# Last half of the rows in two column halves, and its stores on three queues

## The chip, the cores and the metric

The kernel runs on one core of one Trainium2 chip. The metric is device time of one execution in microseconds (us); less is better. Five engines run side by side and wait for each other by semaphores: TensorE (PE, matrix products; PEld are its weight loads), VectorE (DVE), ScalarE (ACT), GpSimd (POOL) and SyncE (SP, which only issues DMAs). ACT and POOL can issue DMAs too. All DMAs are carried by sixteen DMA engines.

## The reference

Two transformer layers in float32 on 256 rows of width 2048: a hybrid block (a matrix-memory LSTM and a gated delta rule) and then an attention block (differential attention and neighbourhood attention). What matters here is the very end of the second block:

```python
mixed = jnp.concatenate([oa, ob], axis=-1) @ w_out[layer]
h = h + gate[:, None] * mixed
return rmsnorm(h, final_g)
```

`mixed` is a product of 256 x 2048 by 2048 x 2048. `gate` is one number for each of the 2048 columns. `rmsnorm` divides each row by the root of its mean square over all 2048 columns, so no output of a row can be scaled before the whole row is there, and multiplies by `final_g`, one number for each column.

## The kernel before

The 256 rows are two halves `t` of 128 rows, which lie on the 128 partitions. The 2048 output columns are four blocks `n` of 512. The depth of 2048 is sixteen tiles `kt` of 128. Products are exact to float32 by splitting both operands into a high and a low part (`hi`, `lo`, type fp32r): each product is three TensorE instructions, high by high, high by low and low by high. The weight block of one `n` is loaded in eight pieces `q` of two depth tiles by `load_w` (lines 131 to 143): SyncE fetches the raw piece, ACT writes `hi` (line 139), DVE writes `lo` (line 140).

Column blocks 0 to 2 go through `proj` (lines 161 to 174): each piece is used for both row halves at once, so both are done at the same time. For block 3 (lines 1437 to 1455) all eight pieces of the weights are kept, five of them in buffers named `kept`, and each row half has a PSUM tile `pL` of 512 columns and 48 products of its own (16 depth tiles times three): first half `t = 0`, then `t = 1`. The first half's tail then runs while TensorE does the second half.

The tail of one row half is two functions. `last` (lines 1391 to 1397) multiplies the PSUM result by the gate (DVE, 1395), adds the residual (DVE, 1396) and squares the sum on ACT with a running total into one column of `s3t` (1397), a column for each block `n`. `store` (1399 to 1413) adds the four totals (DVE, 1402), turns them into a mean (DVE, 1403), takes the power -0.5 on POOL (`pow_`, line 178), and scales the four blocks of 512 columns by it: blocks 0 and 1 on ACT (1412), block 2 on DVE (1410), block 3 on DVE with `final_g` in the same instruction (1408; the others were multiplied by it before). Each block is stored by a DMA of 128 x 512 numbers, 256 KB, from SyncE (1413).

The order of the instructions on an engine is not that of the code: a scheduler sets it, with its own estimate of times, from the dependences. In the program before, it puts some products of the second row half among those of the first, where weights of the first are not ready by its estimate, and lets the stores leave in the order 2, 0, 1, 3. Each engine then keeps to its order.

Of the kernel before, what the change touches and what calls it, by code (L numbers as in the profile page):

```python
# [9 lines left out]
F32 = mybir.dt.float32  # L10
F32R = mybir.dt.float32r
AF = mybir.ActivationFunctionType
ALU = mybir.AluOpType
# [3 lines left out]
P = 128  # L17
D = 2048
T = 256
KT = D // P  # L20
# [64 lines left out]
def hybrid_block_kernel(  # L85
# [3 lines left out]
    nc = tc.nc  # L89
    act, ve, pe, gp = nc.scalar, nc.vector, nc.tensor, nc.gpsimd  # L90
    out = out[0]
# [10 lines left out]
    small = ctx.enter_context(tc.tile_pool(name="small", bufs=2))  # L102

    def side(shape=(P, 512), name="s"):
        return psB.tile(list(shape), F32, tag="s", name=name)
# [25 lines left out]
    def load_w(src, nk, ncol, hilo=None):  # L131
        raw = wraw.tile([P, nk, ncol], F32, tag="w", name="w")
        nc.sync.dma_start(raw, src)
        return split_w(raw, nk, ncol, hilo)

    def split_w(raw, nk, ncol, hilo=None):
        hi, lo = hilo or (wsp.tile([P, nk, ncol], F32R, tag=tg, name=tg) for tg in ("hi", "lo"))
        with tc.high_priority(offset=100):
            act.activation(hi, raw, AF.Copy)  # L139
            last_lo[0] = ve.tensor_tensor(lo, raw, hi.bitcast(F32), ALU.subtract)  # L140
        if tick[0] is not None:
            tick[0]()
        return hi, lo

    def proj_T(w, j0, ntiles, acts, name="pT"):

        na = len(acts)
        ps = psA.tile([P, 2, 2, T], F32, tag="p", name=name)
        for j in range(ntiles):
            for h in range(2):  # L150
                hi, lo = load_w(w[j0 + j, h], 8, P)
                for k in range(8):
                    kt = h * 8 + k
                    for a, (xh, xl) in enumerate(acts):
                        o = ps[:, a, j, :] if na == 2 else ps[:, j // 2, j % 2, :]
                        pe.matmul(o, hi[:, k, :], xh[:, kt, :], start=(kt == 0), stop=False)  # L156
                        pe.matmul(o, hi[:, k, :], xl[:, kt, :], start=False, stop=False)  # L157
                        pe.matmul(o, lo[:, k, :], xh[:, kt, :], start=False, stop=(kt == KT - 1))  # L158
        return ps

    def proj(w, n, acts, name="pN", qs=range(8), pss=None):

        pss = pss or [psA.tile([P, 2, 512], F32, tag="p", name=name) for _ in acts]
        for q in qs:
            hi, lo = load_w(w[n, q], 2, 512)
            for ps, (xh, xl) in zip(pss, acts):
                for t in range(2):
                    s = slice(t * P, (t + 1) * P)
                    for k in range(2):
                        kt = q * 2 + k  # L170
                        pe.matmul(ps[:, t, :], xh[:, kt, s], hi[:, k, :], start=(kt == 0), stop=False)  # L171
                        pe.matmul(ps[:, t, :], xh[:, kt, s], lo[:, k, :], start=False, stop=False)  # L172
                        pe.matmul(ps[:, t, :], xl[:, kt, s], hi[:, k, :], start=False, stop=(kt == KT - 1))  # L173
        return pss

    def pow_(o, i, e):

        gp.tensor_tensor(o, i, e, ALU.pow)
# [21 lines left out]
    with ExitStack() as b1:  # L200
# [17 lines left out]
        with ExitStack() as s0:  # L218
# [64 lines left out]
            for w in range(2):  # L283
                for j in (1, 3):
                    for h in range(2):
                        hl = load_w(d["dn_qkv"][J0[w] + j, h], 8, P)
                        o = ps0[w][:, j // 2, j % 2, :]
                        for k in range(8):
                            kt = h * 8 + k
# [50 lines left out]
        with s1:  # L340
            nc.sync.dma_start(raws, d["if_ba"])
            ps = side([P, T], name="ps")[0:48]
            for h in range(2):
                hi, lo = split_w(raws[:, h * 8:(h + 1) * 8, :], 8, 48)
                for k in range(8):
                    kt = h * 8 + k
# [20 lines left out]
            e = gpool.tile([P, 2, 24], F32, name="e")  # L367
# [118 lines left out]
        def gate_row(n):  # L486

            gate = macc[8 + n][0]
            bm = modp[0].tile([P, 512], F32, tag="m", name="bm", bufs=4)
            nc.sync.dma_start(bm, d["b_mod"][(8 + n) * 512:(9 + n) * 512].partition_broadcast(P))  # L490
            ps = side(name="ms")
            pe.matmul(ps, ones, gate, start=True, stop=True)
            ve.tensor_tensor(gate, bm, ps, ALU.add)
            return gate
# [14 lines left out]
        def mods_all(upto):  # L509
            while mod_next[0] < upto:  # L510
                mod_step(mod_next[0])
                mod_next[0] += 1
# [6 lines left out]
        with ExitStack() as s2:  # L519
# [44 lines left out]
            for hg in range(4):  # L564
                vv, ww = (dn.tile([P, 2, 4, P], F32, tag=nm, name=nm) for nm in ("vv", "ww"))
                kq = dk.tile([P, 4, 2, T], F32, tag="kq", name="kq")
                ps = kps0 if hg == 0 else proj_T(d["dn_qkv"], 16 + 4 * hg, 4, U)
                rows = rsb if hg == 0 else None
                conv_silu(ps, 16 + 4 * hg, kq[:, :, 0, :], rows)
                ps = qps0 if hg == 0 else proj_T(d["dn_qkv"], 4 * hg, 4, U)  # L570
# [63 lines left out]
                ps = proj_T(d["dn_qkv"], 32 + 4 * hg, 4, U)  # L634
# [93 lines left out]
                for t in range(2):  # L728
                    for h in range(4):
                        s = gz[:, t, h * P:(h + 1) * P]  # L730
# [15 lines left out]
        with ExitStack() as s3:  # L746
# [3 lines left out]
            for hg in range(2):  # L750
                kq = dk.tile([P, 4, 2, T], F32, tag="kq", name="kq")
                kT, qT = kq[:, :, 0, :], kq[:, :, 1, :]
                ps = proj_T(d["ml_k"], 4 * hg, 4, U)
                act.activation(kT, ps.rearrange("p a b t -> p (a b) t"), AF.Copy)  # L754
                ps = proj_T(d["ml_q"], 4 * hg, 4, U)
                act.activation(qT, ps.rearrange("p a b t -> p (a b) t"), AF.Copy, scale=P ** -0.5)
                for hp_ in range(2):
# [58 lines left out]
                    for b in range(2):  # L816
# [4 lines left out]
                        for j in range(2):  # L821
                            k = 4 * (2 * hg + hp_) + 2 * b + j
# [10 lines left out]
        hf = [hfp.tile([P, 2, 512], F32, tag="hf", name="hf", bufs=4) for _ in range(4)]  # L833
# [30 lines left out]
        with ExitStack() as s4:  # L864
# [66 lines left out]
            for n in range(4):  # L931
# [3 lines left out]
                for kk in range(4):  # L935
                    ps = side([P, T], name="ps")
                    for t in range(2):
                        pe.transpose(ps[:, t * P:(t + 1) * P], xs[:, t, kk * P:(kk + 1) * P], ident)
                    k = 4 * n + kk
# [10 lines left out]
    with ExitStack() as b2:  # L950
# [201 lines left out]
        a2 = b2.enter_context(tc.tile_pool(name="a2", bufs=2, reuse_waits="tile"))  # L1152
# [233 lines left out]

        M = [(Cat(mah, mbh), Cat(mal, mbl))]
        hf = []
        s3t = small.tile([P, 2, 4], F32, tag="s3t", name="s3t")
        r3 = small.tile([P, 2], F32, tag="r3", name="r3")  # L1390
        def last(ps, t, n, gate):

            h_ = hf[n][:, t, :]
            y = a2.tile([P, 512], F32, tag="e", bufs=3, name="y")
            ve.tensor_tensor(y, ps, gate, ALU.mult)
            ve.tensor_tensor(h_, h_, y, ALU.add)
            act.activation(y, h_, AF.Square, accum_out=s3t[:, t, n:n + 1])

        def store(t, fw):

            r = r3[:, t:t + 1]
            ve.tensor_reduce(r, s3t[:, t, :], AX.X, ALU.add)
            ve.tensor_scalar(r, r, 1.0 / D, 1e-6, ALU.mult, ALU.add)
            pow_(r, r, mh[:, 0:1])
            for n in range(4):
                h_ = hf[n][:, t, :]
                if n == 3:
                    ve.scalar_tensor_tensor(h_, h_, r, fw, ALU.mult, ALU.mult)
                elif n == 2:
                    ve.tensor_scalar(h_, h_, r, None, ALU.mult)  # L1410
                else:
                    act.activation(h_, h_, AF.Copy, scale=r)
                nc.sync.dma_start(out[t * P:(t + 1) * P, n * 512:(n + 1) * 512], h_)


        early = [proj(d["out2"], n, M, qs=range(4)) for n in range(2)]
# [2 lines left out]
        for n in range(4):  # L1419
            fw = a2.tile([P, 512], F32, tag="e", bufs=3, name="fg")  # L1420
            act.dma_start(fw, d["final_g"][n * 512:(n + 1) * 512].partition_broadcast(P))
            if n % 2 == 0:
                hv = a2.tile([P, 2, 2, 512], F32, tag="V", name="hv")
            hf.append(hv[:, n % 2])
            act.dma_start(hf[n], hd[n])
            for t in range(2):
                act.activation(hf[n][:, t, :], hf[n][:, t, :], AF.Copy, scale=r1[:, t:t + 1])
            mods_all(128 + 16 * (n + 1))
            gate = gate_row(n)
            if n < 3:  # L1430
                ps = early[n][0] if n < 2 else proj(d["out2"], n, M)[0]
                for t in range(2):
                    last(ps[:, t, :], t, n, gate)
                    gp.tensor_tensor(hf[n][:, t, :], hf[n][:, t, :], fw, ALU.mult)
                continue

            kept = []
            for _ in range(2):
                kv_ = a2.tile([P, 2, 2, 2, 512], F32R, tag="kT", name="kept")
                kept += [(kv_[:, i, 0], kv_[:, i, 1]) for i in range(2)]  # L1440
            qv = a2.tile([P, 2, 2, 512], F32R, tag="qT", name="kept", bufs=1)
            kept.append((qv[:, 0], qv[:, 1]))
            ws = [load_w(d["out2"][n, q], 2, 512, kept[q] if q < 5 else None) for q in range(8)]
            mh_, ml_ = M[0]
            for t in range(2):
                s = slice(t * P, (t + 1) * P)
                ps = side(name="pL")
                for q, (hi, lo) in enumerate(ws):
                    for k in range(2):
                        kt = q * 2 + k  # L1450
                        pe.matmul(ps, mh_[:, kt, s], hi[:, k, :], start=(kt == 0), stop=False)  # L1451
                        pe.matmul(ps, mh_[:, kt, s], lo[:, k, :], start=False, stop=False)
                        pe.matmul(ps, ml_[:, kt, s], hi[:, k, :], start=False, stop=(kt == KT - 1))
                last(ps, t, n, gate)
                store(t, fw)


# [54 lines left out]
```

## Time and profile before

| | |
|---|---|
| three runs | 1937.52, 1931.1, 1936.2 us |
| median | 1936.2 us |
| the profiled execution's own time | 1928.47 us |
| its span, first to last instruction | 1926.6 us |
| mean granted TensorE clock | 0.995 |
| TensorE busy | 1892.6 us, 98% of the span |
| VectorE busy | 1491.6 us, 77% |
| ScalarE busy | 928.7 us, 48% |
| GpSimd busy | 256.7 us, 13% |

Busy shares are averages over the whole span. Matrix products are pipelined: one begins while the one before is still on its way, so the distance of their starts, and not the length of one, is what they cost. Times in the rows are microseconds from the span's start. A DMA has three moments: its issue on a queue, its data's time on the sixteen engines, and its landing, when the semaphore is told.

### The profile page before, as it was taken

What the parts mean: (1) busy time and instruction counts of PE and PEld (TensorE: products, weight loads), DVE (VectorE), ACT (ScalarE), POOL (GpSimd) and SP (SyncE); (2) the same over time, 40 slices, a digit from 0 to 9 for tenths busy, and PEclk for the clock granted to TensorE, in tenths of its full rate; (3) what the DMA queues carried; (4) which work ended last, traced back from release to release, by engine and by line L of the source; (5) the groups of instructions that cost most, each with busy time, mean ns of one, the idle gap of its engine ahead of it and who ended that gap; (6) DMA issues with size and microseconds to landing.
All of it is one profiled execution on the core that took longest, in us unless ns stands there. A gap on an engine that the chain in (4) does not pass through costs nothing. (4 is left out here: it accounts for less than half of the span.)

```text
span 1926.6 us, 31678 instructions
## 1 busy us (share of the span) xinstructions
PE 1892.6 (98%) x12358; PEld 1676.7 (87%) x12358; DVE 1491.6 (77%) x2141; ACT 928.7 (48%) x1240; POOL 256.7 (13%) x371
## 2 busy tenths in 40 slices
PE   9999999999999999999999999999999999999997
PEld 9989898999878898888888887889999998988776
DVE  6978687684648999879995558698787768878976
ACT  7645444453434443444444356663333355555553
POOL 1011010101101221112120000000000023301311
PEclk9999999999999999999999999999999999999999
DMA  8555454454545778768887576663343387557975
GB/s 294 168 165 169 153 169 155 143 176 137 164 158 198 240 258 264 242 222 266 283 284 245 194 258 227 199 212 116 126 148 120 122 288 204 166 174 256 300 248 178
DMA packets 123974, 389.76 MB, mean 202 GB/s; under 512 B 15408, under 2 KB 21976, under 8 KB 123312
## 3 DMA queue, kind: packets, MB, share of 16 engines
q1 hardware_dynamic: 95296, 314.44, 48.7%
q0 software_dynamic: 19296, 54.19, 9.7%
q10 hardware_dynamic: 9232, 19.11, 2.9%
q8 instruction: 97, 1.59, 0.3%
q14 instruction: 53, 0.43, 0.1%
HBM read 368.50 MB, written 16.03 MB: 200 GB/s over the span
## 5 line engine op out<-in xcount | busy, mean ns | idle before, releaser
L139 ACT ACTIVATE hi<-w 128x1024 fp32r<-128x1024 f32 (+1 forms) x535 | 559.1, 1047 | 711.3 <-PE pN L173 393.5
L140 DVE TENSOR_TENSOR lo<-w,hi 128x1024 fp32r<-128x1024 f32 (+1 forms) x535 | 647.7, 1213 | 266.1 <-ACT hi L139 256.7
L172 PE MATMUL pN<-lo,uh 128*128 128x512 f32 x768 | 306.2, 399 | 0.0
L171 PE MATMUL pN<-hi,uh 128*128 128x512 f32 x768 | 304.7, 397 | 0.0
L173 PE MATMUL pN<-hi,ul 128*128 128x512 f32 x768 | 304.5, 396 | 0.0
L156 PE MATMUL pT<-uh,hi 128*128 128x256 f32 x896 | 255.5, 285 | 2.2 <-ACT kq L754 1.9
L158 PE MATMUL pT<-uh,lo 128*128 128x256 f32 x896 | 256.5, 286 | 0.0
L157 PE MATMUL pT<-ul,hi 128*128 128x256 f32 x896 | 255.7, 285 | 0.0
L171 PEld LDWEIGHTS pN<-hi,uh 128*128 128x128 f32 x768 | 145.0, 189 | 33.8
L173 PEld LDWEIGHTS pN<-hi,ul 128*128 128x128 f32 x768 | 145.0, 189 | 33.2
L172 PEld LDWEIGHTS pN<-lo,uh 128*128 128x128 f32 x768 | 145.1, 189 | 33.1
L156 PEld LDWEIGHTS pT<-uh,hi 128*128 128x128 f32 x896 | 168.7, 188 | 5.2 <-ACT kq L754 2.1
L158 PEld LDWEIGHTS pT<-uh,lo 128*128 128x128 f32 x896 | 168.8, 188 | 2.9 <-issue 2.4
L473 DVE SCALAR_TENSOR_TENSOR ma<-m,sc,ma 128x512 f32<-128x512 f32 x240 | 171.1, 749 | 0.0
L157 PEld LDWEIGHTS pT<-ul,hi 128*128 128x128 f32 x896 | 168.8, 188 | 1.8 <-issue 1.2
L463 POOL DMA_DIRECT2D m<-in_w_mod_dram x128 | 69.5, 543 | 287.7 <-DVE ma L473 206.1
L139 ACT ACTIVATE hi<-TT 128x1024 fp32r<-128x1024 f32 x56 | 59.6, 1065 | 77.2 <-PE pK L1064 54.6
L140 DVE TENSOR_TENSOR lo<-TT,hi 128x1024 fp32r<-128x1024 f32 x56 | 68.4, 1223 | 21.0 <-ACT hi L139 20.6
L156 PE MATMUL pT<-hxh,hi 128*128 128x256 f32 x256 | 73.7, 288 | 1.8 <-ACT ra L1165 1.8
L157 PE MATMUL pT<-hxl,hi 128*128 128x256 f32 x256 | 73.0, 285 | 0.0
L158 PE MATMUL pT<-hxh,lo 128*128 128x256 f32 x256 | 73.0, 285 | 0.0
L172 PE MATMUL pN<-lo,hxh 128*128 128x512 f32 x160 | 63.7, 398 | 1.9 <-DVE lo L140 1.8
(729 smaller groups left out, 4053.1 us busy)
## 6 DMA issues: line engine op xcount, KB each, us to landing
w<-in_dn_qkv_dram SPq DMA_DIRECT2D x88, 512.0 KB, 3.2
m<-in_w_mod_dram POOLq DMA_DIRECT2D x128, 256.0 KB, 4.1
w<-in_dn_z_dram SPq DMA_DIRECT2D x32, 512.0 KB, 3.2
w<-in_ml_v_dram SPq DMA_DIRECT2D x32, 512.0 KB, 3.8
w<-in_ml_z_dram SPq DMA_DIRECT2D x32, 512.0 KB, 4.2
w<-in_ml_o_dram SPq DMA_DIRECT2D x32, 512.0 KB, 4.1
w<-in_gate_a_dram SPq DMA_DIRECT2D x32, 512.0 KB, 4.4
w<-in_gate_b_dram SPq DMA_DIRECT2D x32, 512.0 KB, 4.4
```

The lines of the kernel that those rows point to most:

```text
L139: act.activation(hi, raw, AF.Copy)
L140: last_lo[0] = ve.tensor_tensor(lo, raw, hi.bitcast(F32), ALU.subtract)
L156: pe.matmul(o, hi[:, k, :], xh[:, kt, :], start=(kt == 0), stop=False)
L157: pe.matmul(o, hi[:, k, :], xl[:, kt, :], start=False, stop=False)
L158: pe.matmul(o, lo[:, k, :], xh[:, kt, :], start=False, stop=(kt == KT - 1))
L171: pe.matmul(ps[:, t, :], xh[:, kt, s], hi[:, k, :], start=(kt == 0), stop=False)
L172: pe.matmul(ps[:, t, :], xh[:, kt, s], lo[:, k, :], start=False, stop=False)
L173: pe.matmul(ps[:, t, :], xl[:, kt, s], hi[:, k, :], start=False, stop=(kt == KT - 1))
L463: (gp if g < 8 else nc.sync).dma_start(raw, d["w_mod"][g, kt])
L473: ve.scalar_tensor_tensor(a, raw, s, a, ALU.mult, ALU.add)
```

## The change

The second half of the rows (`t = 1`) of column block 3 is done in two halves of 256 columns, each with a PSUM tile, 48 products and a call of `last` of its own; the left half comes first in the code. `s3t` has five columns instead of four for each row half: the right half of `t = 1` writes the fifth, and GpSimd clears it at the start, since the first row half doesn't write it. In `store` the four blocks are scaled in the code's order 2, 0, 3, 1, and their DMAs are issued by SyncE (2 and 3), ACT (0) and POOL (1). This holds for both row halves.

```diff
-        s3t = small.tile([P, 2, 4], F32, tag="s3t", name="s3t")
+        s3t = small.tile([P, 2, 5], F32, tag="s3t", name="s3t")
+        gp.memset(s3t[:, :, 4:5], 0.0)
...
-        def last(ps, t, n, gate):
+        def last(ps, t, n, gate, cols=slice(0, 512), i=None):
...
-            h_ = hf[n][:, t, :]
-            y = a2.tile([P, 512], F32, tag="e", bufs=3, name="y")
-            ve.tensor_tensor(y, ps, gate, ALU.mult)
+            h_ = hf[n][:, t, cols]
+            y = a2.tile([P, 512], F32, tag="e", bufs=3, name="y")[:, cols]
+            ve.tensor_tensor(y, ps, gate[:, cols], ALU.mult)
             ve.tensor_tensor(h_, h_, y, ALU.add)
-            act.activation(y, h_, AF.Square, accum_out=s3t[:, t, n:n + 1])
+            i = n if i is None else i
+            act.activation(y, h_, AF.Square, accum_out=s3t[:, t, i:i + 1])
...
-            for n in range(4):
+            for n, q in ((2, nc.sync), (0, act), (3, nc.sync), (1, gp)):
...
-                nc.sync.dma_start(out[t * P:(t + 1) * P, n * 512:(n + 1) * 512], h_)
+                q.dma_start(out[t * P:(t + 1) * P, n * 512:(n + 1) * 512], h_)
...
-                ps = side(name="pL")
-                for q, (hi, lo) in enumerate(ws):
-                    for k in range(2):
-                        kt = q * 2 + k
-                        pe.matmul(ps, mh_[:, kt, s], hi[:, k, :], start=(kt == 0), stop=False)
...
-                last(ps, t, n, gate)
+                for c in range(t + 1):
+                    cols = slice(c * T, (c + 1) * T) if t else slice(0, 512)
+                    ps = side(name="pL")[:, cols]
+                    for q, (hi, lo) in enumerate(ws):
+                        for k in range(2):
+                            kt = q * 2 + k
+                            pe.matmul(ps, mh_[:, kt, s], hi[:, k, cols], start=(kt == 0), stop=False)
...
+                    last(ps, t, n, gate, cols, n + c)
                 store(t, fw)
```

What this does to the order on the engines stands in the two built programs. First TensorE, of the changed program, around the last products of the first row half (512 columns; `pL` is the PSUM tile, `mah`, `mal` and `mb` the activations, `kept`, `hi` and `lo` the weights), lines 1457 to 1459 being the three products:

```order
L1457 MATMUL pL<-hi,mb 128x512
L1458 MATMUL pL<-kept,mah 128x256
L1458 MATMUL pL<-lo,mb 128x512
L1459 MATMUL pL<-hi,mb 128x512
L1457 MATMUL pL<-hi,mb 128x512
L1458 MATMUL pL<-lo,mb 128x512
L1459 MATMUL pL<-hi,mb 128x512
L1459 MATMUL pL<-kept,mal 128x256
L1457 MATMUL pL<-kept,mah 128x256
```

Products of the left column half (128x256) still stand among those of the first row half, 14 of them; after its last one come the other 34 of the left half and then the 48 of the right. No product of the right half comes earlier.

Then VectorE at the end of the program, before (-) and now (+), with what a row waits for:

```order
-L1395 TENSOR_TENSOR y<-pL,mr 128x512 [waits PE_49]
-L1396 TENSOR_TENSOR hv<-hv,y 128x512 [waits DVE_49]
-L1402 TENSOR_REDUCE r_18136<-s3t 128x1 [waits Activation_49]
...
+L1396 TENSOR_TENSOR y<-pL,mr 128x256 [waits PE_49]
+L1397 TENSOR_TENSOR hv<-hv,y 128x256 [waits DVE_49]
+L1396 TENSOR_TENSOR y<-pL,mr 128x256 [waits PE_49]
+L1397 TENSOR_TENSOR hv<-hv,y 128x256 [waits DVE_49]
+L1404 TENSOR_REDUCE r_18137<-s3t 128x1 [waits Activation_49]
```

Two pairs of 256 columns stand where one of 512 stood, behind the scaling of the first row half.

Last the issuing engines: GpSimd's end of the program, before and now (`r` is the root, `hv` the rows to store):

```order
-L178 TENSOR_TENSOR r_18136<-r_18136,mh 128x1 x2
-L1508 UNCONDITIONAL_BRANCH
-L1508 ISA
...
+L178 TENSOR_TENSOR r_18137<-r_18137,mh 128x1
+L1416 DMA out_dram<-hv 128x512
+L178 TENSOR_TENSOR r_18137<-r_18137,mh 128x1
+L1416 DMA out_dram<-hv 128x512
```

The first row half's store now stands between the two roots. On ScalarE a store follows both scalings of its row half, and SyncE keeps four stores of eight. On the other engines' earlier rows nothing but line numbers differs; on GpSimd the clearing of `s3t` comes among the first instructions of the program.

## Rows read from the trace of the kernel before

**Rows 1.** Stages of the program's end: busy time of each engine, PEclk, DMA share, GB/s.

```profile
1895.31:1917.30 21.99, 21.99 (x96) 17.64 (x94) 11.31 (x16) 7.65 (x12) 3.63 (x3) 1.00 0.35 124
1917.30:1920.56 3.26, 0.00 (x1) 0.00 (x0) 1.69 (x4) 0.72 (x3) 0.56 (x1) 0.97 0.00 0
1920.56:1924.72 4.16, 0.00 (x0) 0.00 (x0) 1.15 (x2) 1.33 (x2) 0.00 (x0) 0.50 0.68 252
```

**Rows 2.** Timeline of PE: start, length, engine, line, operation; second and last product of block 3.

```profile
1895.31 0.39 PE L1452 MATMUL pL<-kept,mah 128*128 128x512 f32 x1
...
1916.90 0.40 PE L1453 MATMUL pL<-hi,mb 128*128 128x512 f32 x1
```

**Rows 3.** Timeline of all engines behind the last product.

```profile
1917.34 0.69 DVE L1395 TENSOR_TENSOR y<-pL,mr 128x512 f32<-128x512 f32 x1 [4.04 <-PE pL L1453]
1918.06 0.69 DVE L1396 TENSOR_TENSOR hv<-hv,y 128x512 f32<-128x512 f32 x1
1918.79 0.63 ACT L1397 ACTIVATE y<-hv 128x512 f32<-128x512 f32 x1 [5.30 <-DVE hv L1396]
1919.32 0.19 ACT L1397 ACTIVATION_READ_ACCUMULATOR y<-hv 128x1 f32 x1
...
1920.56 1.34 ACT L1412 ACTIVATE hv<-hv,r 128x512 f32<-128x512 f32 x2 [1.05 <-POOL r L178]
1920.56 0.49 DVE L1410 TENSOR_SCALAR hv<-hv,r 128x512 f32<-128x512 f32 x1 [0.67 <-POOL r L178]
1920.96 0.74 DVE L1408 SCALAR_TENSOR_TENSOR hv<-hv,r,fg 128x512 f32<-128x512 f32 x1
```

**Rows 4.** Timeline of PE in two stretches with products of 256 columns.

```profile
1420.23 0.28 PE L1063 MATMUL pK<-s4h,hi 128*128 128x256 f32 x1
...
1423.97 0.28 PE L1065 MATMUL pK<-s1h,lo 128*128 128x256 f32 x1
...
501.29 0.27 PE L158 MATMUL pT<-uh,lo 128*128 128x256 f32 x1
...
502.95 0.28 PE L157 MATMUL pT<-ul,hi 128*128 128x256 f32 x1
```

**Rows 5.** Groups by line and form, DVE, 256 columns: busy us, mean ns of one.

```profile
L1083 DVE TENSOR_TENSOR stg<-pK,tm 128x256 f32<-128x256 f32 x8 | 3.4, 423 | 0.2
...
L801 DVE TENSOR_TENSOR hv<-np__7252,gz 128x256 f32<-128x256 f32 x1 | 0.4, 415 | 0.0
```

**Rows 6.** Timeline of ACT: a square of 256 columns with its sum.

```profile
624.72 0.39 ACT L799 ACTIVATE hv<-np__6682 128x256 f32<-128x256 f32 x1
625.00 0.19 ACT L799 ACTIVATION_READ_ACCUMULATOR hv<-np__6682 128x1 f32 x1
```

**Rows 7.** DMA engines' busy tenths from 1921 to 1922, in 40 slices.

```profile
DMA  0000000000000000000000000000000000009469
```

**Rows 8.** Stage within the last stores; columns as in rows 1.

```profile
1922.60:1923.30 0.70, 0.00 (x0) 0.00 (x0) 0.00 (x0) 0.00 (x0) 0.00 (x0) 0.50 1.03 383
```

**Rows 9.** The last four stores, line 1413: issue ns min/median/max, first and last issue, landing.

```profile
L1413 SPq DMA_DIRECT2D out_dram<-hv x4: 333/386/413, 1921.1 to 1922.5; - x4
...
DMA to landing us min/median/max: 2.1/2.5/2.8
```

**Rows 10.** Stores of 256 KB that GpSimd issues, line 1132: time to landing.

```profile
DMA to landing us min/median/max: 2.5/3.1/7.2
```

**Rows 11.** Timeline of DVE: the low part of block 3's sixth weight piece.

```profile
1899.69 1.22 DVE L140 TENSOR_TENSOR lo<-w,hi 128x1024 fp32r<-128x1024 f32 x1
```

**Rows 12.** Timeline of PE: 256-column products behind an idle stretch.

```profile
1601.37 0.38 PE L156 MATMUL pT<-hxh,hi 128*128 128x256 f32 x1 [1.79 <-ACT ra L1165]
...
1603.08 0.41 PE L157 MATMUL pT<-hxl,hi 128*128 128x256 f32 x1
...
1603.93 0.41 PE L158 MATMUL pT<-hxh,lo 128*128 128x256 f32 x1
```

**Rows 13.** PE's busy time and granted clock in that stretch.

```profile
1603.10:1604.10 1.00, 1.00 (x6) 0.50 0.99 350
```

More of the change, by code (lines that the diff above doesn't have):

```diff
@@ L1446, in hybrid_block_kernel @@
                 s = slice(t * P, (t + 1) * P)
-                ps = side(name="pL")
-                for q, (hi, lo) in enumerate(ws):
-                    for k in range(2):
-                        kt = q * 2 + k
-                        pe.matmul(ps, mh_[:, kt, s], hi[:, k, :], start=(kt == 0), stop=False)
-                        pe.matmul(ps, mh_[:, kt, s], lo[:, k, :], start=False, stop=False)
-                        pe.matmul(ps, ml_[:, kt, s], hi[:, k, :], start=False, stop=(kt == KT - 1))
-                last(ps, t, n, gate)
+                for c in range(t + 1):
[5 more added lines that the diff above has]
+                            pe.matmul(ps, mh_[:, kt, s], hi[:, k, cols], start=(kt == 0), stop=False)
+                            pe.matmul(ps, mh_[:, kt, s], lo[:, k, cols], start=False, stop=False)
+                            pe.matmul(ps, ml_[:, kt, s], hi[:, k, cols], start=False, stop=(kt == KT - 1))
+                    last(ps, t, n, gate, cols, n + c)
                 store(t, fw)
```

## The prediction

> **What bounds the kernel now.** I read the end of the program first, by stages [rows 1]: all that the change touches lies there. Three stages follow one another. From 1895.31 to 1917.30 us TensorE does the last weight block's 96 products without a gap, at a granted clock of 1.00, the 2.4 GHz level. From 1917.30 to 1920.56 it is idle, and one short chain runs over VectorE, ScalarE and GpSimd until the second half of the rows has its root. From 1920.56 to 1924.72 four stores of 256 KB go out. Another 1.88 us (1924.72 to the span's end, 1926.6) belong to landing and the program's close. The change can take time only from 31.3 us.
>
> Then the timeline inside each stage. The products start 0.2297 us apart: 94 steps from 1895.31 to 1916.90 [rows 2]. In the chain [rows 3] gate product, residual sum and square each wait for the one before, each over 512 columns: their starts lie 0.72 and 0.73 us apart, and the square with the reading of its sum takes 0.72 (1918.79 to 1919.51). At 1920.56 both scaling engines start: VectorE ends column block 2 at 1921.05 and block 3 at 1921.70, ScalarE ends block 0 near 1921.28 and block 1 at 1921.90.
>
> Last the transfers. The first store is issued at 1921.07, right behind the first scaled block, and its data moves from 1921.90 [rows 7]: 0.83 us. From there on the sixteen DMA engines are full, share 1.03 at 383 GB/s [rows 8], and 1 MB at that rate is 2.74 us, which ends at 1924.64; the window before puts it near 1924.7. So the stores are held by the engines, not by the queue.
>
> **TensorE.** 48 products of 512 columns become 96 of 256 for the second half of the rows; the first half keeps its 48. Of the same form as the new ones are the products of line 1063 to 1065: 32 steps from 1420.23 to 1423.97, 0.1169 us each; another stretch has 14 steps in 1.66 us, 0.1186 [rows 4]. From the first product's start to the last's it is now 95 x 0.2297 = 21.82 us. Afterwards 48 x 0.2297 + 95 x 0.1169 = 22.13. The last product itself takes 0.28 instead of 0.40 [rows 2, 4]. Sum: +0.31 - 0.12 = **+0.19 us**, with 0.1186 +0.35. I take the longer stretch; the lower end is -0.12, if two halves cost just one whole.
>
> The scheduler still mixes the second half's products into the first's, to fill waits for weights. Fewer columns fill now, so a weight piece could come too late. I laid the new order along these steps: the tightest place is the low part of the sixth of eight pieces, ready at 1900.91 [rows 11] and first used near 1903.37. Margin 2.5 us, no stall; cost nothing.
>
> **The chain.** Gate product, sum and square of the left 256 columns run while TensorE does the right ones, over 5 us earlier; on VectorE and ScalarE they stand behind the first half's scaling, which is over some microseconds after that half's last product. Cost nothing: the cover is the 5.6 us of the last 48 products, and without it the left half's chain would come on top, the 2.4 us of the right one at most. Behind the last product only 256 columns remain. VectorE's product from PSUM takes 0.423 in line 1083 and one from SBUF 0.415 in line 801 [rows 5], against 0.69 each [rows 3]: -0.27 twice. ScalarE's square with the reading of its sum runs from 624.72 to 625.19 at 256 columns [rows 6], 0.47 against 0.72: -0.25. The reduction reads five numbers instead of four, and the root stays. Sum **-0.79 us**. The ends: -0.54 if ScalarE gains nothing, -0.99 if all three halve (0.36, 0.36, and half of the square's 0.53 before its sum is read).
>
> **The stores.** All of it shifts by 0.19 - 0.79 = -0.60. The first store keeps its place behind block 2, so data starts at 1921.30. To lose nothing, the next 256 KB must be fed every 0.68 us. ScalarE's store of block 0 stands behind both its scalings: issued at 1921.30 at worst, data at 1922.13, just behind the first store's end at 1921.98; with block 3 from SyncE issued at 1921.12 (data 1921.95) there is no gap. Block 1 now goes out by GpSimd, issued at 1921.30; three stores last to 1923.35, so it has two microseconds to start. GpSimd's own stores of 256 KB land 2.5 us after issue at best, 3.1 in the median [rows 10], SyncE's four here 2.1 to 2.8 [rows 9]. Of SyncE's best, 2.1, 0.83 is the way to the data and 0.68 the data, so 0.59 is the landing; with those two GpSimd's median leaves 3.1 - 0.68 - 0.59 = 1.83 to the data's start, just in time. Hence **nothing gained, nothing lost** beyond the shift: the three queues feed engines that were full. Ends: -0.6 more, were the issue the limit (below), and +3.8, if GpSimd's store lands after 7.2 us, its worst.
>
> The Trainium skill, page "DMA: Bandwidth & Descriptors", section "Latency and other measured facts", speaks against this part: it gives about 0.6 us to the first byte for a hardware-issued DMA and about 1 us for one from GpSimd. By that the block on GpSimd starts 0.4 us later than it would on SyncE; with two microseconds to spare that leaves the sum at -0.60.
>
> The first half's store on GpSimd stands ahead of that engine's second root. It waits for ScalarE's block 1 of that half, some 9 us earlier than the same wait of the second half, so nothing queues behind it; ScalarE's first store likewise goes before the squares of the second half. The clearing of the sums' fifth column is one small instruction among others that the order puts at GpSimd's start: nothing. The sums' buffer grows and moves later buffers; no row prices that, and I take nothing.
>
> **Sum.** -0.60 us on the profiled execution's 1928.47 (span 1926.6 and 1.87 around it): 1927.9. That execution is 7.7 below the median of the runs shown, 1936.2; on the median it gives **1935.6 us**. About 0.3% (5.8 us) is what a measurement of this kernel can tell from no change, so I forecast no measurable change. The edit would have to save most of an idle chain of 3.3 us and more besides to be seen.
>
> **Rivals.**
> - **TensorE's clock drops while the narrow products run (slower).** At 1601.37 TensorE began 256-column products after 1.79 us of idling; soon after, the granted clock was 0.50, the 1.2 GHz level, and four steps from 1603.08 to 1603.93 were 0.2125 each [rows 12, 13]. In this stage that costs 96 x (0.2125 - 0.1169) = +9.2, so 1936.2 - 0.6 + 9.2 = 1944.8. It decides if the engine idles here as it did there. Against it: the margin of 2.5 us, and 32 such products in a row at the full step [rows 4]. Chance 0.03.
> - **GpSimd's store lands last.** The three others' data ends at 1923.35, so nothing hides a late one. With the worst landing, 7.2 [rows 10], it comes at 1928.5 instead of about 1925.3 (1922.5 + 2.8 [rows 9]): +3.2, 1939.4. Against it: the median, 3.1, gives 1924.4. Chance 0.13.
> - **The issue limits after all.** Four issues lie 1921.07 to 1922.5 apart on one queue, and the last block's landing hangs on the last issue. Now the last issue is at 1921.30, 1.2 earlier; with 2.8 to landing the program ends 1.2 earlier, 1935.0. Against it: full engines [rows 8]. By the Trainium skill, "DMA: Bandwidth & Descriptors", section "Issuing engines are not separate DMA queues", several issuing engines save only the issue time; the trace, with a share of 1.03, makes that saving worth nothing. Chance 0.10.
> - **The order is not what the edit says**, with right columns before left, or the first half of the rows held back. The built order shows the left half's last product 48 ahead of the end, so I give this nothing of its own.
>
> **How the numbers follow.** Forecast 0.70, late store 0.13, issue 0.10, clock 0.03, and 0.04 for what no row prices, the moved buffers above all, half to each side. The first three lie within 0.3% of the median: 0.93, of which I leave 0.01 to chance on the fast side. So faster 0.03, same 0.92, slower 0.05. The range reaches from 1928.0, the forecast on the fastest execution shown (1927.9), to 1939.5, the late store on the median (1939.4); the clock's case is left out. The runs themselves, 1931.1 to 1937.5, lie inside.
>
> **What would show it.** Right: 256-column starts 0.117 to 0.119 apart at a granted clock of 1.00; the idle chain 2.4 to 2.6 us long instead of 3.26; the first store's data 0.83 behind its issue; DMA share near 1.0 for 2.7 us; GpSimd's store landing within 3.1 us. Wrong: a step near 0.21, an idle TensorE inside the stage, a gap in the DMA share before the fourth block, or a change in any stage before 1895 us.

## The result, and the profile after

| kernel | median us | runs | ratio to before, 95% interval |
|---|---|---|---|
| before, beside it | 1934.16 (1931.1 to 1937.52) | 4 | |
| changed | 1914.51 (1912.93 to 1917.14) | 4 | 0.9902 (0.9887 to 0.9916) |

The change is 19.7 us faster, far outside the forecast range, whose lower end was 1928.0. The profiled execution took 1914.26 us.

The page of the changed kernel, first its span and the busy times:

```profile
span 1912.1 us, 31776 instructions
...
PE 1872.1 (98%) x12406; PEld 1665.0 (87%) x12406; DVE 1491.9 (78%) x2143; ACT 929.5 (49%) x1242; POOL 264.1 (14%) x374
```

The same line of the kernel before:

```profile
PE 1892.6 (98%) x12358; PEld 1676.7 (87%) x12358; DVE 1491.6 (77%) x2141; ACT 928.7 (48%) x1240; POOL 256.7 (13%) x371
```

TensorE has 48 products more and is busy 20.5 us less. The edit touches the last 33 us, so this cannot come from there alone. Both programs give TensorE the same products in the same order until close to the end, so the starts can be laid side by side, product by product: the changed kernel is ahead by 2.0 us at 78 us, 4.2 at 163, 7.8 at 307, 13.7 at 828 and 16.6 at 1056. The time is won in small pieces all the way through. The mean granted clock of the two profiled executions doesn't explain it: 0.995 before, 0.994 in the change.

Two stages show how. The stretch at 130 us is a run of products of 256 columns (activations `uh`, `ul` against weights, lines 156 to 158); that at 899 is a run of products of 512 columns (lines 171 to 173). Window, PE busy (count), granted clock, DMA share, GB/s, in the kernel before:

```profile
130.20:163.20 33.00, 33.00 (x281) 1.00 0.61 189
...
899.20:1024.20 125.00, 125.00 (x540) 1.00 0.85 277
```

and the same work in the changed one:

```profile
127.50:160.50 33.00, 33.00 (x293) 1.00 0.61 201
...
884.30:1009.30 125.00, 125.00 (x548) 1.00 0.84 279
```

TensorE never idles in either, the granted clock is 1.00 in both, and yet 33 us hold 293 products instead of 281, and 125 us 548 instead of 540. Over the whole of the first run, 321 steps (its first, longer one left out), the mean step from start to start falls from 118.7 ns to 113.4; over 562 steps of the second, counted in the same way, from 232.4 to 228.9. One group goes the other way. Line 172 with the activations `hah`: durations min/median/max, first and last start; before, then changed:

```profile
L172 PE MATMUL pN<-lo,hah x128: 389/389/389, 1042.1 to 1128.4; 128*128 128x512 f32 x128
```

```profile
L172 PE MATMUL pN<-lo,hah x128: 393/396/398, 1025.1 to 1114.0; 128*128 128x512 f32 x128
```

Its stage takes 88.9 us instead of 86.3. So the engine is not faster in general: which products gain and which lose depends on their operands.

Now the end, where the edit is. The stages that answer to [rows 1] and, in the last line, to [rows 8]:

```profile
1878.78:1901.20 22.42, 22.35 (x144) 20.16 (x142) 13.59 (x19) 8.22 (x15) 4.75 (x4) 1.00 0.35 126
1901.20:1903.67 2.47, 0.00 (x0) 0.00 (x0) 1.13 (x4) 0.51 (x2) 0.58 (x1) 1.00 0.00 0
1903.67:1907.92 4.25, 0.00 (x0) 0.00 (x0) 1.15 (x2) 1.33 (x2) 0.60 (x1) 0.64 0.66 247
1905.70:1906.40 0.70, 0.00 (x0) 0.00 (x0) 0.00 (x0) 0.00 (x0) 0.20 (x1) 0.50 1.05 392
```

TensorE's idle stretch is 2.54 us instead of 3.26: its last product ends at 1901.13, 0.07 us ahead of the second stage shown. The stores again fill the DMA engines (1.05). But from 1907.92, where the data ends, to the span's end it is 4.2 us instead of 1.88. The timeline behind the last product, beside [rows 3] and [rows 9]:

```profile
1901.62 0.42 DVE L1397 TENSOR_TENSOR hv<-hv,y 128x256 f32<-128x256 f32 x1
1902.08 0.42 ACT L1399 ACTIVATE y<-hv 128x256 f32<-128x256 f32 x1 [4.75 <-DVE hv L1397]
...
1902.62 0.16 DVE L1404 TENSOR_REDUCE r<-s3t 128x1 f32<-128x5 f32 x1 [0.57 <-ACT y L1399]
...
1903.06 0.58 POOL L178 TENSOR_TENSOR r<-r,mh 128x1 f32<-128x1 f32 x1 [5.96 <-DVE r L1405]
...
1903.67 0.49 DVE L1413 TENSOR_SCALAR hv<-hv,r 128x512 f32<-128x512 f32 x1 [0.70 <-POOL r L178]
...
1904.18 0.99 SPq L1416 DMA_DIRECT2D out_dram<-hv  x2
1904.42 0.35 ACTq L1416 DMA_DIRECT2D out_dram<-hv  x1
1905.30 0.60 POOL L1416 DMA_DIRECT2D out_dram<-hv  x1 [1.66 <-ACT hv L1415]
```

GpSimd issues the last store and is done with that at 1905.90. What it does then stands in the rows of the program's closing line: the engine's queue, the operation, durations in ns min/median/max, first and last start. Changed kernel, then before:

```profile
L1514 POOLq DRAIN  x3: 51/98/6007, 1905.3 to 1911.8; - x3
L1514 SPq DRAIN  x3: 7/7/7, 1908.8 to 1911.5; - x3
```

```profile
L1508 POOLq DRAIN  x3: 51/98/5833, 1919.9 to 1926.3; - x3
L1508 SPq DRAIN  x3: 7/7/7, 1925.5 to 1926.0; - x3
```

A long drain of GpSimd, about 6 us, begins with its last instruction in both. Before, that instruction is the root, the drain runs from 1919.93 to 1925.76, and SyncE, which waits for its stores, is done at 1925.5: nearly a tie. In the changed kernel SyncE is done at 1908.8, and GpSimd drains until 1911.3.

### The profile page after: what moved, and what is told of

It is laid out like the page before. It is cut to its first block, busy times and chain, and to the rows that moved or that the text cites. A ratio compares the mean times of both kernels' runs of the same rounds, so it can differ in the third digit from the quotient of the medians.

```text
span 1912.1 us, 31776 instructions
## 1 busy us (share of the span) xinstructions
PE 1872.1 (98%) x12406; PEld 1665.0 (87%) x12406; DVE 1491.9 (78%) x2143; ACT 929.5 (49%) x1242; POOL 264.1 (14%) x374
```

## The experiments

In the expectations theory A is that the gain comes from the buffers' places: `s3t` with five columns takes 40 bytes of a partition instead of 32, a buffer is padded to 64, there are two, and so every buffer allotted after it stands 64 bytes further. Its rivals were the edited end itself (B) and any change of the order of instructions (C). A1 is the form of A by which only the place of the activations against the weights counts. Theory D is that GpSimd's drain sets the close. Places below are bytes modulo 256, read from the built programs: in the kernel before the weight pieces `hi` and `lo`, and the raw ones they are made from, stand at 0, `uh`, `ul` and `hxh` at 128, `hah` at 0. The activations are allotted behind `s3t` and move with it; these weights are not.

**1. The buffers alone moved.** The kernel before, order unchanged:

```diff
-        s3t = small.tile([P, 2, 4], F32, tag="s3t", name="s3t")
+        s3t = small.tile([P, 2, 5], F32, tag="s3t", name="s3t")[:, :, 0:4]
```

> The kernel before, with nothing changed but the size of the buffer of the sums (five columns allotted, four used), which moves all large activation buffers by 64 bytes per partition, as in the change; the order of instructions is that of before. Theory A (the gain is where the buffers lie: TensorE's products start closer together when the activations are moved): 0.985 to 0.995 of the time before, about 1914 to 1919 us, and the products of line 172 in the stage with uh step at 226 to 230 ns instead of 232. Theory B (the gain is in the edited end: column halves and three queues): the time of before within 0.2%, 1934 us, step 232 ns. Theory C (any change of the instruction stream): as B.

1915.13 us (4 runs), ratio 0.9902 (0.9885 to 0.9918): all of the change's gain, with none of its instructions. The two stages, columns as above:

```profile
127.90:160.90 33.00, 33.00 (x294) 1.00 0.60 199
...
885.40:1010.40 125.00, 125.00 (x548) 1.00 0.86 281
```

Also `hah` is slower as in the change: 88.9 us (1026.2 to 1115.1). Both rivals fall.

**2. The edit without the move.** The changed kernel, with its ten sums and the root in one tile, so that the later buffers stay:

```diff
-        s3t = small.tile([P, 2, 5], F32, tag="s3t", name="s3t")
+        m3 = small.tile([P, 16], F32, tag="s3t", name="m3")
+        s3t = m3[:, 0:10].rearrange("p (t c) -> p t c", t=2)
...
-        r3 = small.tile([P, 2], F32, tag="r3", name="r3")
+        r3 = m3[:, 10:12]
```

> The changed kernel, with the nine sums and the two roots put into one buffer of the old size, so that every large buffer lies where it lay before; column halves, queues and order of stores as in the change. Theory A: the time of before less 0.6 us by my sum, about 1933.5 us, ratio 0.9985 to 1.0005, and the step 232 ns as before. Theories B and C: the time of the change, about 1914.5 us, ratio 0.990.

1935.74 us (10 runs), ratio 1.0015 (1.0004 to 1.0027). The stages are those of the kernel before:

```profile
129.80:162.80 33.00, 33.00 (x280) 1.00 0.60 192
...
900.70:1025.70 125.00, 125.00 (x540) 1.00 0.84 278
```

What was edited on purpose makes the kernel slightly slower, more than I expected: its end, from the second product of block 3 to the span's end, takes 33.37 us instead of 31.25, which is 0.0011 of the whole.

**3. Everything moved, weights too.** The kernel before, with a constant that is allotted ahead of all large buffers:

```diff
-    w1 = const.tile([P, 1], F32, name="w1")
+    w1 = const.tile([P, 24], F32, name="w1")[:, 0:1]
```

> The kernel before with one early one-number buffer widened, so that every large buffer moves by 64 bytes: the weights' pieces too, not the activations alone. Same order of instructions. Theory A1 (what counts is how stationary and moving operand lie to each other): the time of before, 1934 us, lines 171 to 173 with uh stepping at 232 ns and with hah at 226 to 227. Theory A2 (the place of the activations alone counts): as the move by 64 alone, 1915 us, steps 226 to 232 with uh and 233 with hah.

1935.73 us (10 runs), ratio 1.0002 (0.9985 to 1.0019), the median steps as before (232 and 119 ns):

```profile
129.80:162.80 33.00, 33.00 (x280) 1.00 0.61 194
...
899.40:1024.40 125.00, 125.00 (x537) 1.00 0.85 276
```

So moving all of them does nothing for the time; what counts is the place of the activations against what stayed in experiment 1 and moves here: the weights, split and raw (A1). The places don't fix every step, though. The 512-column products with `uh` have two mean steps, 232.4 and 233.3 ns, and keep one of them over a whole stretch: before, it is 233.3 from 750 to 898 us and 232.4 from 899 on; here it is the other way round, hence the 537 products in place of 540.

**4. Other distances.** The kernel before with `s3t` made larger, or a small filled tile in a pool of its own in front of the activations; weights unmoved:

```diff
-        s3t = small.tile([P, 2, 4], F32, tag="s3t", name="s3t")
+        s3t = small.tile([P, 2, 12], F32, tag="s3t", name="s3t")[:, :, 0:4]
...
     small = ctx.enter_context(tc.tile_pool(name="small", bufs=2))
+    pad = ctx.enter_context(tc.tile_pool(name="pad", bufs=1))
+    gp.memset(pad.tile([P, 8], F32, name="pad"), 0.0)
```

12 columns give 128 bytes, 16 give 192, 24 give 320; a pad of 8 numbers gives 32, one of 24 gives 96.

> The kernel before with the buffer of the sums wide enough to move the activation buffers by 128 bytes. Theory A in its form that the place within 256 bytes counts: uh then lies as hah lay before, whose products stepped at 226 to 227 ns, and hah as uh lay (232 ns); the sum is some 0.985 to 0.990 of before, 1905 to 1915 us, most of it in the stages with uh. In its form that only the place within 128 bytes counts: the time of before, 1934 us. B and C: the time of before.

> The kernel before with the activation buffers moved by 192 bytes. Theory A by 256 bytes: uh lies as hah lay in the change, whose products stepped at 233 ns; ratio 0.998 to 1.004, 1930 to 1942 us. By 128 bytes: as the move by 64, about 1914 to 1919 us. B and C: the time of before.

> The activation buffers moved by 32 bytes, one memset more on GpSimd. If the place counts in steps of 64 bytes only: steps as before (232 ns with uh in line 172, 119 to 120 in line 156). If finer: steps between those of no move and of 64 (226 and 114), time 1915 to 1934 us.

> The activation buffers moved by 96 bytes. If steps of 64 count: as the move by 64 (226 ns in line 172, 114 in line 156), 1915 us. If finer: between the move by 64 and by 128 (227 and 120).

> The kernel before with its activations 320 bytes further: 64 more than a multiple of 256. Period of 256: the steps and the time of the move by 64, about 1915 us, line 172 at 226 ns and line 156 at 114 ns with uh. Period of 512: other steps, as in no run so far.

Median steps from start to start in ns, worked out from the traces' starts (lines 171, 172, 173 in that order; one number where all agree within 1):

| moved by | median us, ratio | 512 columns, `uh` | 512 columns, `hah` | 256 columns, `uh` |
|---|---|---|---|---|
| 0 (before) | | 232 | 226 to 227 | 119 to 120 |
| 32 | 1936.37, one run | 231 to 232 | 233 to 234 | 117 to 118 |
| 64 (exp. 1) | 1915.13, 0.9902 | 232, 226, 229 | 233.5, 233, 232 | 113 to 114 |
| 96 | 1938.61, one run | 234 | 234 | 117 |
| 128 | 1924.52, 0.9954 (0.9941 to 0.9967) | 227 | 231 to 232 | 120 |
| 192 | 1928.9, 0.9969 (0.9958 to 0.9981) | 233 to 234 | 232, 226, 229 | 118 |
| 320 | 1916.2, one run | 232, 226, 229 | 233.5, 233.5, 231 | 113 to 114 |

The medians of the kernel before beside these runs were 1934.19 (32 and 96: 1933.64; 320: 1931.19). Three things follow. 320 does what 64 does, so the pattern repeats after 256 bytes, where that was tried. The columns `uh` and `hah` tell the same story half a period apart: at place 0 both take 227 (`hah` unmoved, `uh` moved by 128), at 128 both 232, at 192 both 232, 226, 229, and at 64 both about 233. And the form with 256 columns, where the weights are the stationary operand, has its best place, 192, where the other form has nearly its best: that is where the change happened to put `uh`. I had expected 1905 to 1915 for the move by 128; it missed, since the 256-column products gained nothing there. For the move by 192 I had expected 0.998 to 1.004, and its gain is a little larger. For the move by 32 I had 1915 to 1934 us, were the grain finer than 64, and for 96 a time and steps between those of 64 and 128. In single runs neither gained; the 256-column steps lie between those of the neighbouring places, the 512-column ones with 96 above both.

The medians hide that here too a place allows two steps. In the change and in experiment 1 the long stretches of 256-column products with `uh` step by 113.3 to 113.4 ns, but one of them, 366.4 to 405.1 us in the change, by 117.8, with the same operands in the same places at a granted clock of 1.00. `hxh`, at the same place modulo 256 as `uh`, steps by 117.8 as well. What chooses between the two, no run here shows.

**5. One weight part moved.** The changed kernel with the buffers of `hi` and `lo` in two pools and 64 bytes between them, block 1 stored by ScalarE (the tile of experiment 2 holds the sums):

```diff
+    wpad = ctx.enter_context(tc.tile_pool(name="wpad", bufs=1))
+    gp.memset(wpad.tile([P, 16], F32, name="wpad"), 0.0)
+    wsl = ctx.enter_context(tc.tile_pool(name="wsl", bufs=3))
...
-        hi, lo = hilo or (wsp.tile([P, nk, ncol], F32R, tag=tg, name=tg) for tg in ("hi", "lo"))
+        hi, lo = hilo or ((wsp if tg == "hi" else wsl).tile([P, nk, ncol], F32R, tag=tg, name=tg) for tg in ("hi", "lo"))
```

> As the change with block 1 stored from ScalarE, activations 64 bytes further, and the low parts of the weights (the buffers lo) 64 bytes further too, the high parts not. If the places of stationary and moving operand to each other count product by product (A1), the products with hi alone keep the steps of the change (114 ns for line 156, 226 to 232 for 512 columns) and only products next to a low part change: line 158's place at 256 columns moves toward 119 to 120 (low part and activations now 128 apart).

One run, 1928.6 us against 1932.11 before. A surprise: with `lo` moved, the 256-column products of `hi` (lines 156 and 157) went back to 119 to 120 ns, though neither of their own operands stood otherwise against the other; line 158, with `lo`, took 116. So A1 product by product is wrong: the place of `lo` counts for products that don't read it. Whether it acts through the neighbouring products, which read `lo`, or through VectorE, which writes it, was not found.

With 128 bytes between them, and the activations at 192 as in the change:

> The same with the low parts 128 bytes further, 64 from the activations the other way. By A1 line 158's place at 256 columns moves toward 118, the others stay.

> The version of e12 (column halves, block 1 stored from ScalarE, activations 192 and low parts 128 bytes past a multiple of 256) in five rounds. By A1 and D together it should be under the change: ratio 0.987 to 0.990 of before, about 1908 to 1914 us. If e12's single time was chance, the ratio of the change, 0.990 to 0.992.

> As f1, but the activations another 256 bytes further (448 becomes 192 past a multiple of 512). If places count to a multiple of 256 bytes: the steps of e12 (line 172's place 229 ns with uh, line 156's place 113 to 114 with uh and with hxh). If to a multiple of 512: with uh like the change (226, 232, 229), with hxh 117.

The first gave 1912.97 us in one run; the same kernel again, in 6 runs, 1916.74, ratio 0.9912 (0.9891 to 0.9933); with the activations 256 bytes further 1911.84 in one run. The 512-column steps are 229, 229, 230, and 256-column steps with the activations `hxh` fall to 113 to 114 as well (117 in the change), as does the one slower stretch with `uh`. Line 158 stayed at 113 to 114, where the first of these three forecasts had it move toward 118: A1 product by product misses again. Still the repeated kernel's time is not below the change's, against my expectation of 0.987 to 0.990; it is what I had written for the case that the first time was chance. The waits of TensorE from 1740 to 1890 us show part of why: waiting instruction, releaser, us in total, times, longest; the repeated kernel, then the one with the activations moved on:

```profile
PE tp L1232 <- ACT e L1331: 5.9, 3, 3.4
PE pN L172 <- DVE lo L140: 4.3, 4, 1.5
```

```profile
PE pN L172 <- DVE lo L140: 3.1, 3, 1.3
...
PE tp L1232 <- ACT e L1331: 1.3, 2, 1.1
```

Before, the wait of line 1232 took 2.3 us and that of line 172 3.0. Summed over the products from 1582 us to near the end, TensorE idled 12.1 us before, 14.4 in the change, 16.9 in experiment 1, 21.4 in the repeated kernel and 13.8 in its neighbour: a faster TensorE runs into weights and exponentials that are not ready sooner. Executions of one kernel differ by about as much as these sums do (1913.1 to 1919.86 for the repeated one), so that this takes the rest of the gain is likely, not shown.

**6. The stores alone.** The kernel before with three queues and the new order:

```diff
-            for n in range(4):
+            for n, q in ((2, nc.sync), (0, act), (3, nc.sync), (1, gp)):
...
-                nc.sync.dma_start(out[t * P:(t + 1) * P, n * 512:(n + 1) * 512], h_)
+                q.dma_start(out[t * P:(t + 1) * P, n * 512:(n + 1) * 512], h_)
```

> The kernel before with the stores on three queues and in the order 2, 0, 3, 1, and nothing else. From the start of the last scaling to the span's end it took 6.00 us before and 8.41 in the change. Theory D (the program's close waits for GpSimd, which needs over 5 us from its last instruction until it reports): 8.3 to 8.5 us here, so about 2.4 us slower at the end, and the stores land within 0.1 us of before. Theory E (the longer close comes from the column halves or from the smaller blocks): 6.0 us here.

One run, 1935.98 us (1933.64 before). From the first scaling to the span's end it takes 8.40 us, 6.00 before, and the closing rows say why:

```profile
L1508 POOLq DRAIN  x3: 51/98/6005, 1927.2 to 1933.7; - x3
L1508 SPq DRAIN  x3: 7/7/7, 1930.7 to 1933.5; - x3
```

The last store had landed 4.78 us after the first scaling's start (4.70 before), and SyncE was done at 1930.7. GpSimd's drain, begun at 1927.2 with its store instead of at 1924.98 with the root, ends only at 1933.2 and with it the program.

**7. The change without GpSimd's store.**

```diff
-            for n, q in ((2, nc.sync), (0, act), (3, nc.sync), (1, gp)):
+            for n, q in ((2, nc.sync), (0, act), (3, nc.sync), (1, act)):
```

> The change with column block 1 stored from ScalarE's queue instead of GpSimd's, all else as in the change, buffers moved by 64 bytes. Theory D (the close waits for GpSimd): from the start of the last scaling to the span's end 6.0 to 6.3 us instead of 8.41, the whole end from the second product of block 3 about 30.9 instead of 33.3, time some 2.4 us under the change, ratio to before 0.989. Theory E (the close is longer for another reason, such as stores on several queues): 8.4 us and the ratio of the change, 0.990.

> As before this one, but with the buffers at their old places. By theories A1 and D together: steps as before (232 ns in line 172's place with uh), and the end 0.3 us shorter than before's 31.25, about 30.95 us from the second product of block 3.

In the trace it does what D says: 6.00 us from the first scaling, and the whole end 30.88 us instead of the change's 33.30. The drain begins behind the root again:

```profile
L1514 POOLq DRAIN  x3: 51/98/5833, 1911.0 to 1917.4; - x3
L1514 SPq DRAIN  x3: 7/7/7, 1916.5 to 1917.1; - x3
```

The time does not show it: 1915.89 us (5 runs), ratio 0.9909 (0.9894 to 0.9924), where I expected 0.989. A gain of 2.4 us is 0.0013, less than the interval's half. The same edit on experiment 2 gave 1931.7 us in one run (before 1932.11) and an end of 30.96 us.

**8. The columns alone.** Experiment 2 with the stores as they were, `((0, nc.sync), (1, nc.sync), (2, nc.sync), (3, nc.sync))`.

> The column halves alone, with the stores all on SyncE as before and all buffers at their old places. From the second product of block 3 to the span's end: 31.25 us before, 33.3 in the change. By the sum of what was seen (products +0.56, start of the chain -0.11, chain -0.72 us) and a close of 6.0 as before: 30.9 to 31.0 us. If column halves lengthen the close, 33.3.

One run, 1929.38 us (before 1931.19); the end takes 31.01 us instead of 31.25, with 6.00 from the first scaling.

No version beat the change clearly; experiments 5 and 7 have intervals that overlap its own.

## Why the prediction was wrong

**The step that failed** is the sentence "The sums' buffer grows and moves later buffers; no row prices that, and I take nothing". It was worth -20 us: experiment 1 has all of the ratio 0.9902 by that move alone, experiment 2 none of it without. I gave it a share of 0.04, half to each side, and no size. A row did hint at a price: [rows 4] show 256-column steps of 0.1169 us with one pair of operands and 0.1186 with another at the same granted clock, and I used the difference only to choose between them. Had I asked why two products of one shape differ, the 1.5% between them over 1893 us of TensorE's work would have been a bound of some 27 us to either side. My own mark for being wrong, "a change in any stage before 1895 us", is what came.

The gain, from the mean steps before and after (waits of over 1 us left out): 2,304 products of 512 columns with `uh` -7.3 us, 2,688 of 256 columns with `uh` -8.6, 768 of 256 with `hxh` -3.6, 384 with `hbh` -2.8, 384 with `hah` +2.5. That is -19.8 of the 20.5 us by which PE is less busy. Nearly half of the -2.8 is not the place: in the profiled execution of before, nine of those products ran at a granted clock of 0.50, 426 to 427 ns apart; without them it is -1.5.

**The second step that failed** is "nothing gained, nothing lost" for the stores. The transfers themselves did what it says: the last landing is 4.79 us behind the first scaling instead of 4.70, with GpSimd's store not late (4.79 - 1.63 = 3.16 from its issue; the median of [rows 10] is 3.1). But I carried the 1.88 us behind the last data over as fixed. They hang on GpSimd's drain, and so on GpSimd's last instruction, which the change moves from the root to a store: +2.41 us. No rival had that mechanism; the one with a late store from GpSimd named the right engine and a like price (+3.2) for another reason.

**The end, term by term**, the profiled executions of before and after:

| term | predicted | measured |
|---|---|---|
| products, first start to last | +0.31 | +0.48 |
| last product to the chain's start | -0.12 | -0.12 |
| chain | -0.79 | -0.72 |
| stores and close | 0 | +2.41 |
| sum | -0.60 | +2.05 |

The products were mis-sized: 0.1169 us was the step of other operands. A stretch of the new ones in the changed kernel:

```profile
1895.24 0.28 PE L1457 MATMUL pL<-kept,mah 128*128 128x256 f32 x1
...
1897.88 0.28 PE L1458 MATMUL pL<-kept,mah 128*128 128x256 f32 x1
```

22 steps in 2.64 us, 0.120 each; over all 95 it is 0.1183, close to the other value that I had, 0.1186. With that the first two terms were +0.35 together in place of +0.19, and +0.36 was measured. The chain was right in mechanism and within 0.1 in size.

**The rivals.** The clock did not drop: 1.00 in the stage of the products, with no idle time in it after the block's start. The issue did not limit: the last one came 1.63 us after the scaling's start instead of 1.90, and the last landing came no earlier (4.79 instead of 4.70), as the full engines (1.05) had it. The Trainium skill, page "DMA: Bandwidth & Descriptors", section "Issuing engines are not separate DMA queues", says that starting DMAs from several engines saves only the time that it takes to issue them, and this trace agrees: the issue came 0.27 us earlier, the landing did not. And in experiments 7 and 8 stores on two queues and on one both end 6.00 us after the first scaling. The order was as the edit says.

## What to carry to other kernels

An edit that changes the size of a buffer can move all that are allotted after it; on a kernel whose TensorE is never idle, first lay the steps of one product before and after side by side far from the edit, and time the edit once with the old places and the old code once with the new ones, before a gain is put down to the edit. Two products of one shape with different steps at one granted clock were such a sign here, and are a reason to try a few paddings of 64 bytes on purpose. The program's close can hang on the engine that finishes its own queue last: here a last store on GpSimd made the close 2.4 us longer in the traces (experiments 6 and 7), too little to show in the times.

## What was not expected of the hardware

- The step of a product depends on the place of the activations against the weights, modulo 256 bytes, at a granted clock of 1.00: median steps of 226 to 234 ns with 512 columns, 113 to 120 with 256. Moving both by the same 64 bytes leaves the medians and the time (232 and 119, ratio 1.0002), moving the activations alone changes the kernel's time by 1% (0.9902). Moves by 32 and 96 bytes gave no gain, in one run each.
- It depends also on the place of a buffer that it does not read: moving `lo` by 64 bytes took the products of `hi` from 114 to 119 to 120 ns.
- At one place a long stretch can keep either of two steps: 113.4 or 117.8 ns with 256 columns (the change), 232.4 or 233.3 with 512 (the kernel before). What inside the memory or the engine causes all this no run here shows.
- GpSimd's drain at the program's close ends 5.2 to 5.4 us after its last instruction's end (5.24 behind the root, 5.39 behind a store), and the program waits for it: its span ended 8.40 us behind the first scaling with that store and 6.00 without it.
